# A list scheduler that knows of the SBUF port, of longer scans and of longer matmuls

## The chip, the cores and the metric

The kernel runs on one core of one Trainium2 chip. The metric is the device time of one execution in microseconds; the time before is the median of three runs. The profile is of one more execution on the same kind of chip, taken with the hardware profiler.

## The reference, cut to what matters

Four layers of one trunk over 256 context tokens and 256 latent tokens, model width 1024, all in float32. Each layer has two sub-layers:

```
hg, rw, gates = split(modulate(rms_norm(x), shift, scale) @ w_in)   # 2560 + 1920 + 2048 columns
o_hg = bidirectional HGRN2 (gated linear recurrence, 4 heads of 128)
o_rw = bidirectional RWKV-7 (decay, delta-rule state update, 8 heads of 64, grid-aware token shift)
m = sigmoid(g_hg) * (o_hg @ proj_a) + sigmoid(g_rw) * (o_rw @ proj_b)
x = x + gate * rms_norm(m @ w_out)
x = x + gate * rms_norm((silu(h @ w1_gate) * (h @ w1_up)) @ w2)     # SwiGLU, 2816 wide
```

The shifts, scales and gates come from `silu(c) @ ada_w` (adaLN modulation), for the latent and for the context condition. The recurrences of the context start from zero, and those of the latent tokens from the context's final states. The output is the latent stream after four layers; in the last layer the context goes only as far as its states.

## The kernel before, in words

Activations lie channel-major, 128 channels by 512 tokens (context, then latent) in a tile. A float32 product is made of three fast ones: weights and activations are each split into a rounded part (`wh`, `hh`) and the rest (`wl`, `hl`), and `mm3` adds wh x hh, wh x hl and wl x hh in PSUM. Weights come from DRAM in pieces of 128x512 (`wr`); ScalarE (ACT) makes `wh`, and GpSimd (POOL) or VectorE (DVE) makes `wl = wr - wh`.

In the mixing stage several streams run together: for each of four pairs of RWKV heads a preparation (`rw_pair`), a solver of unit triangular matrices (`rw_solve`: 30 steps on VectorE with tiles `XS` and `S`, then small matmuls) and a state chain over eight chunks (`rw_chain`: c_ps matmuls, `S0P` on GpSimd, updates of `UV` and `S` on VectorE); for each of four HGRN2 heads seven levels of a decay tree (`hg_head`: `hX`, `hY` on VectorE, `SF`, `PF`, `PB`, `SB` on GpSimd); and the gate projections. Then come the merge, the output projection and SwiGLU, big matmuls with simple work around them. The modulation of the next layer (`ada_pair`: sums of 128x512 products on VectorE) is spread over that.

The order of the instructions is not written by hand. `body` records every instruction in a `Plan`: a node with its engine (or "any": VectorE or GpSimd), what it must wait for, and a cost in nanoseconds from `Plan.cost`. `Plan.schedule` then runs a list schedule over five queues (pe, act, vec, pool, dma): at each step the engine that can start first takes, of its ready nodes, the one with the highest rank (the longest chain of costs and lags that hangs on it, plus a bias of its stream); `LOOK` lets an engine wait shortly for a better node. `emit` issues the instructions in the order of their planned starts, and on the chip every engine runs its own list in that order. `PAR` (when each stream is recorded), `BIAS` and `LOOK` are constants that were chosen for this kernel. The costs that matter here, before:

```python
# pe, float32r operands; n columns of output, m of weights
return max(n / 2.4, m / 1.2) + 2.5
# vec
two = name in ("tensor_scalar", "tensor_copy") and not psum
return 67.0 + n * (0.53 if two else 1.042) + 61.0 * ptr
# pool, tensor_scalar with a scalar from memory
return 686.0
```

Nothing in the plan before says that VectorE and GpSimd can hold each other up.

Of the kernel before, what the change touches and what calls it, by code (L numbers as in the profile page):

```python
# [14 lines left out]
PSUM = bass.MemoryType.PSUM  # L15

P = 128
D = 1024
NK = 8
T = 512  # L20
# [51 lines left out]
MAXLOOK = 200  # L72
WINDOW, COLD = 4096 / 1.2, (0.39, 0.87)
# [10 lines left out]
class Node:  # L84
    """One instruction, or several of an engine in a row, with what it waits for."""
# [3 lines left out]
    def __init__(self, engs, calls, preds, costs, load, kind):  # L89
        self.engs, self.calls, self.preds, self.costs, self.load, self.kind = engs, calls, preds, costs, load, kind  # L90


class Plan:
    """Takes down the kernel's instructions, and emits them in the order of a list schedule: each engine runs, of what
    could start, what the longest chain of work hangs on."""
# [10 lines left out]
    def lo(self, i):  # L106
        """The engine of the weights' second parts."""
        return self.any if LO[i] else self.pool

    def tile(self, pool, shape, dt, tag, bufs, name):  # L110
        """A tile; one of a tag takes the place of the one that its tag gave out bufs tiles before."""
        if not tag:
            t = pool.tile(shape, dt, name=name)
            self.tiles[t.tensor.name] = ([], [], ())
            return t
        t = pool.tile(shape, dt, tag=tag, name=name, bufs=bufs)
        held = self.tags.setdefault((id(pool), tag), [])
        held.append(t.tensor.name)
        old = self.tiles.pop(held.pop(0)) if len(held) > bufs else ([], [])
        self.tiles[t.tensor.name] = ([], [], {x for x, _ in old[0] + old[1]})  # L120
        return t

    @staticmethod
    def region(a):
        """Partitions and elements that an access pattern spans."""
        ap, off = a.ap, a.offset
        sp = str(a.space)
        if sp.endswith("PSUM"):
            return 0, 128, 0, 1
        if sp.endswith("SB"):  # L130
            row, n = ap[0]
            p0, off, rest = off // row, off % row, ap[1:]
        else:
            p0, n, rest = 0, 1, ap
        lo = off + sum(min(0, s * (c - 1)) for s, c in rest)
        hi = off + sum(max(0, s * (c - 1)) for s, c in rest) + 1
        return p0, p0 + n, lo, hi

    def together(self):
        """The instructions recorded in this context, all of one engine, stay one after another."""  # L140
        @contextmanager
        def group():
            self.gang = -1
            yield
            self.gang = None
        return group()

    def add(self, engs, name, args, kw):
# [6 lines left out]
        preds = set()  # L155
# [16 lines left out]
        preds.discard(n)  # L172
        b = 4
# [3 lines left out]
        if join:  # L177
            x = self.nodes[n]
            x.calls.append((name, args, kw))
            x.preds |= preds  # L180
            x.costs[0] += costs[0]
        else:
            load = b / DMA_RATE if engs[0] == "dma" else 0.0
            if engs[0] == "pe":
                load = args[1].ap[0][1] / P * (0.37 if out.start_partition() and out.shape[0] <= C else 1.0)
            self.nodes.append(Node(engs, [(name, args, kw)], preds, costs, load, self.kind))
# [8 lines left out]
    @staticmethod  # L195
    def cost(eng, name, out, args, kw):
        """Nanoseconds that an instruction holds its engine."""
        n = 1
# [7 lines left out]
        if eng == "pe":  # L206
            w = args[1].ap
            m = 1
            for x, c in w[1:]:
                m *= c  # L210
            if name == "transpose":
                return max(m / 1.2, 107.0)
            if args[1].dtype == F32R:
                return max(n / 2.4, m / 1.2) + 2.5
            if m == n and m <= 64:
                return (0.9 if out.start_partition() else 1.75) * m
            n = 2 * n / 2.4 * (0.44 if n == 512 and out.ap[0][1] == 32 else 1.0)
            return 2 * (max(n, m / 1.2) + 2.5)
        if eng == "act":
            return (51.0 if psum else 93.0) + n * 0.833 + 93.0 * bool(ptr)  # L220
        if eng == "vec":
            if name == "memset":
                return n * 1.05
            two = name in ("tensor_scalar", "tensor_copy") and not psum
            return 67.0 + n * (0.53 if two else 1.042) + 61.0 * ptr
        if name == "memset":
            return 35.0 + 0.833 * n
        if name == "tensor_scalar":
            if ptr:
                return 686.0  # L230
# [10 lines left out]
    def schedule(self):  # L241
# [26 lines left out]
        tail = 1e9  # L268

# [8 lines left out]
        while len(order) < N:  # L278
# [26 lines left out]
            _, i = heapq.heappop(ready[e])  # L305
            x = nodes[i]
            on[i] = e
            c = x.costs[x.engs.index(e)]
# [43 lines left out]
def body(ctx, tc, xT, cc, ada_w, w_in, rw_lo, rw_g2, proj_a, proj_b, w_out, ffn_w1, ffn_w2,  # L352
# [122 lines left out]
    def load_split(src, k0, nk, c0, ncol, place=None):  # L475
        """Weight rows k0*128.. and columns c0.. as its rounded part and the rest."""
# [24 lines left out]
    def psum2(w, src, hi, lo, rg=slice(0, T), tag="s"):  # L501
        """PSUM tile with w^T src for w of zeros and ones, src going in two parts."""
# [7 lines left out]
    def spots(tile):  # L510
        """Places for the split weights of one output tile in [P, 4, T]."""
# [7 lines left out]
    def proj(src, nk, c0, xh, xl, t0, place=None):  # L519
        """PSUM tile with W[:, c0:c0+128]^T x for tokens t0.., with a place for the weights stream by stream."""  # L520
# [24 lines left out]
    def norms(xs, t0, post=None, pre=None):  # L545
        """x += G * rms_norm(y), and then h = rms_norm(x) * A + B per channel and stream, split in two parts."""
# [79 lines left out]
    def ada_put(pm, b, n, ps):  # L626
        """Sums of n blocks of columns from b on, each stream's in 128 / 2 n rows, put channel-major in md."""
# [12 lines left out]
    def ada_first(l, pm):  # L640
        """The first four blocks of 512 columns of silu(c) @ ada_w[l], each in a quarter of the rows."""
# [14 lines left out]
    def ada_pair(l, pm, b):  # L656
        """Blocks b and b + 1, the products summed over the rows of each partition first."""
# [22 lines left out]
    def ada_finish(pm, i):  # L680
        """Scale, shift and gate of sub-layer i // 3 with the norm weights in."""
# [31 lines left out]
    def sigm(o, src, nb, t):  # L713
        """o = sigmoid(src - nb) by exp and ln; t is all of o."""
# [5 lines left out]
    def shifted(ps, j, lmu, t0, tag):  # L720
        """pf = p + mu (shift(p) - p) of projection tile j."""
# [20 lines left out]
    def layer(l, pm, xs, xd, hh, hl):  # L742
# [32 lines left out]
        def stacked(src, tags):  # L775
            """Per direction src's rounded part and the rest, in the two halves of the rows."""
# [204 lines left out]
        def rw_solve(p):  # L981
            """Inverses of pair p's unit triangular matrices, 32 x 32 blocks first."""
# [44 lines left out]
        def rw_chain(p):  # L1027
            """Pair p's state chain, and the outputs of the chunks that both directions have reached."""
# [73 lines left out]
            # group norm  # L1102
# [24 lines left out]
        def hg_head(e):  # L1127
# [55 lines left out]
            def score(h, xx, yy):  # L1183
                """Products of the tokens of a block of 64 with each other or, for h = 64, with the block beside."""
# [105 lines left out]
        def gate_tiles():  # L1290
            """Sigmoids of the gates, to DRAM."""
# [58 lines left out]
        def branch(br, j):  # L1350
            """Branch br's gated part of tile j, and with the second one the sum."""
# [89 lines left out]
    def ada_to(l, i, n=1000):  # L1441
        """At most n more pieces of the modulation, up to the first i parts of layer l."""
# [72 lines left out]
```

## Time and profile before

| | |
|---|---|
| time, median of 3 runs | 4484.12 us (4477.95 to 4488.85) |
| span of the profiled execution | 4491.0 us, which is its own time as far as the page tells; 6.9 us above the median |
| TensorE (PE) busy | 4151.3 us, 92% |
| VectorE (DVE) busy | 3314.2 us, 74% |
| ScalarE (ACT) busy | 2161.3 us, 48% |
| GpSimd (POOL) busy | 2318.9 us, 52% |
| mean granted TensorE clock | 0.924 |

PE is the row of matmuls and PEld that of weight loads, which overlap them. All instructions have one source line, that of `emit` (L341), so groups are told apart by the tiles that they write and read, as `out<-in`. The span's stages, by the times of the weights' transfers and the norms: mixing of layers 0 to 3 in 75 to 676, 1268 to 1892, 2440 to 3063 and 3612 to 4187 us; merge, output projection and SwiGLU between and after them.

### The profile page before, as it was taken

Reading aid. Unit: us, or ns where it says so; the run is one execution under the profiler, and the core shown is the slowest. Engines: PE = TensorE matmul, PEld = TensorE weight load, DVE = VectorE, ACT = ScalarE, POOL = GpSimd, SP = SyncE. Lnnn points to the kernel's source line nnn. Section 1 sums busy time; section 2 is a strip of 40 time slices with the busy share of each in tenths; the row PEclk is TensorE's granted clock in tenths of the full one; section 3 lists DMA queues with packets and bytes.
Section 4 is the critical chain, followed back from the end, with each engine's and each line's share of the span. In section 5 each row is a group of like instructions: output and inputs, shape, how many; then the busy total and the mean of one; then the engine's idle time right before and its main releaser. Section 6 shows DMA issues by size and latency. Waiting matters only on the chain. (4 is left out here: it accounts for less than half of the span.)

```text
span 4491.0 us, 72501 instructions
## 1 busy us (share of the span) xinstructions
PE 4151.3 (92%) x26290; PEld 3248.2 (72%) x26290; DVE 3314.2 (74%) x5772; ACT 2161.3 (48%) x4458; POOL 2318.9 (52%) x2121
## 2 busy tenths in 40 slices
PE   7999998899999999989999999999899989888998
PEld 5676776677777767778777676677777766667888
DVE  5988878977388898676627988876754487887665
ACT  4554653433255565534434554554433354554564
POOL 2464654465445456454654554554555535455542
PEclk8998899999998998899999998899999988887999
DMA  4211127455421111354433211116444421111555
GB/s 151 59 46 36 51 88 227 140 166 158 134 73 57 49 44 46 125 173 125 139 114 122 63 49 41 46 56 205 122 146 124 137 67 43 41 44 39 159 151 162
DMA packets 661415, 451.08 MB, mean 100 GB/s; under 512 B 28224, under 2 KB 584256, under 8 KB 661056
## 3 DMA queue, kind: packets, MB, share of 16 engines
q1 hardware_dynamic: 661056, 446.44, 33.1%
q8 instruction: 207, 3.39, 0.3%
q14 instruction: 152, 1.25, 0.1%
HBM read 416.98 MB, written 29.36 MB: 99 GB/s over the span
## 5 line engine op out<-in xcount | busy, mean ns | idle before, releaser
L341 POOL TENSOR_TENSOR wl<-wr,wh 128x512 fp32r<-128x512 f32 x726 | 1017.5, 1404 | 1034.3 <-ACT wh L341 705.9
L341 PE MATMUL p_ps<-hh,wh 128*128 128x512 f32 (+1 forms) x2784 | 1073.7, 398 | 30.2 <-ACT wh L341 15.8
L341 PE MATMUL p_ps<-hh,wl 128*128 128x512 f32 (+1 forms) x2784 | 1053.1, 397 | 30.9 <-POOL wl L341 21.4
L341 PE MATMUL p_ps<-hl,wh 128*128 128x512 f32 (+1 forms) x2784 | 1060.0, 394 | 0.0
L341 ACT ACTIVATE wh<-wr 128x512 fp32r<-128x512 f32 x986 | 610.0, 621 | 844.3 <-PE p_ps L341 678.8
L341 PEld LDWEIGHTS p_ps<-hh,wl 128*128 128x128 f32 x2784 | 544.5, 198 | 157.8 <-POOL wl L341 46.9
L341 PEld LDWEIGHTS p_ps<-hh,wh 128*128 128x128 f32 x2784 | 541.9, 197 | 145.2 <-ACT wh L341 26.9
L341 PEld LDWEIGHTS p_ps<-hl,wh 128*128 128x128 f32 x2784 | 543.4, 198 | 97.0 <-issue 9.2
L341 POOL TENSOR_SCALAR fn<-fn 128x512 f32<-128x512 f32 (+1 forms) x152 | 230.9, 1519 | 177.4 <-ACT fn L341 168.8
L341 DVE TENSOR_TENSOR fn<-fn,p_ps 128x512 f32<-128x512 f32 (+1 forms) x208 | 127.1, 614 | 219.9 <-ACT fn L341 129.0
L341 POOL TENSOR_SCALAR S0P<-S,pcs 128x64 f32<-128x64 f32 x192 | 156.7, 829 | 222.0 <-DVE S L341 221.2
L341 DVE TENSOR_TENSOR wl<-wr,wh 128x512 fp32r<-128x512 f32 x260 | 186.9, 723 | 101.1 <-ACT wh L341 59.7
L341 DVE TENSOR_TENSOR XS<-XS,S 64x30 f32<-64x30 f32 (+14 forms) x480 | 214.0, 446 | 10.8
L341 ACT ACTIVATE fn<-fn 128x512 f32<-128x512 f32 (+1 forms) x304 | 174.3, 574 | 89.7 <-POOL fn L341 84.9
L341 DVE TENSOR_TENSOR S<-XS 64x30 f32<-64x30 f32 (+14 forms) x480 | 207.3, 432 | 10.8
L341 PE MATMUL s_ps<-XS,X8b 64*64 64x64 f32 (+2 forms) x1024 | 147.2, 298 | 23.2 <-ACT X8a L341 14.5
L341 POOL TENSOR_TENSOR SF<-SF,PF 128x256 f32<-128x256 f32 x112 | 90.9, 812 | 139.0 <-ACT hY L341 138.2
L341 PEld LDWEIGHTS s_ps<-XS,X8b 64*128 64x128 f32 (+1 forms) x1024 | 118.9, 196 | 55.2 <-ACT X8a L341 24.1
L341 PE MATMUL s_ps<-XS,BK 64*64 64x64 f32 (+2 forms) x1024 | 139.2, 275 | 13.3 <-DVE XS L341 12.6
L341 PEld LDWEIGHTS s_ps<-XS,BK 64*128 64x128 f32 (+1 forms) x1024 | 107.9, 175 | 58.9 <-issue 37.1
L341 DVE SCALAR_TENSOR_TENSOR UV<-c_ps,pcs,S0P 64x64 f32<-64x64 f32 x384 | 108.6, 283 | 56.1 <-PE c_ps L341 45.6
L341 PE MATMUL p_ps<-SC,wh 128*128 128x512 f32 (+1 forms) x440 | 143.4, 363 | 2.4 <-ACT SC L341 2.2
(525 smaller groups left out, 9554.7 us busy)
## 6 DMA issues: line engine op xcount, KB each, us to landing
wr<-ffn_w SPq DMA_DIRECT2D x512, 256.0 KB, 3.0
wr<-w_in SPq DMA_DIRECT2D x408, 256.0 KB, 2.9
hq<-ada_w SPq DMA_DIRECT2D x242, 256.0 KB, 2.9
PB<-ada_w SPq DMA_DIRECT2D x110, 256.0 KB, 3.0
wr<-w_out SPq DMA_DIRECT2D x64, 256.0 KB, 3.0
gts<-fn SPq DMA_DIRECT2D x48, 256.0 KB, 3.0
wr<-proj_a SPq DMA_DIRECT2D x32, 256.0 KB, 4.5
wr<-proj_b SPq DMA_DIRECT2D x32, 256.0 KB, 3.8
```

The costliest lines, as they stand in the source:

```text
L341: getattr(self.eng[self.on[i]], name)(*args, **kw)
```

## The change

No instruction is changed. The scheduler's model of time gets new parts. `on_port` marks nodes that use the port to SBUF that VectorE and GpSimd share: on GpSimd tensor_tensor and tensor_copy, on VectorE operations with all operands in SBUF that have two inputs or are a tensor_scalar, copy or transpose. In the schedule such a node begins no sooner than the port is free; where that would be over `PORT` (100 ns) away, the engine looks at up to 12 ready nodes for one that needs no port and ends within `OVER` (200 ns) of the port's release, and takes it first. A VectorE node whose output starts in another group of 32 partitions than the last one's costs 88 ns more. A float32r matmul of 512 columns goes from 215.8 to 228.9 ns, a scan of 512 columns from 600 to 1132, a 1024-column transpose from 1134 to 1193, a GpSimd tensor_scalar with a scalar from memory from 686 to 440. Docstrings and comments are blanked; the lines of the diff that only do that are left out here.

```diff
+PORT, OVER = 100.0, 200.0
...
+    def __init__(self, engs, calls, preds, costs, load, kind, port, quad):
         self.engs, self.calls, self.preds, self.costs, self.load, self.kind = engs, calls, preds, costs, load, kind
+        self.port, self.quad = port, quad
...
+            self.nodes.append(Node(engs, [(name, args, kw)], preds, costs, load, self.kind,
+                                   [self.on_port(e, name, out, args, kw) for e in engs], r[0] // 32 if engs[0] == "vec"
+                                   else None))
...
+    def on_port(eng, name, out, args, kw):
+
+        if eng not in ("vec", "pool"):
+            return False
+        ins = [x for x in (kw.get(k) for k in ("in_", "in0", "in1", "data0", "data1", "data")) if hasattr(x, "space")]
+        ins = ins or [x for x in args[1:] if hasattr(x, "space")]
+        if eng == "pool":
+            return name in ("tensor_tensor", "tensor_copy")
+        if not all(str(x.space).endswith("SB") for x in [out] + ins):
+            return False
+        return len(ins) > 1 or name in ("tensor_scalar", "tensor_copy", "transpose")
...
-                return max(n / 2.4, m / 1.2) + 2.5
+                return max(n / 2.35 + 11.0, m / 1.2 + 2.5)
...
+            if name in ("transpose", "tensor_tensor_scan"):
+                return 67.0 + n * (1.1 if name == "transpose" else 2.08)
...
-                return 686.0
+                return 440.0
...
-            _, i = heapq.heappop(ready[e])
+            r0, i = heapq.heappop(ready[e])
             x = nodes[i]
+            n = x.engs.index(e)
+            if x.port[n] and port > t + PORT:
+                held = [(r0, i)]
+                while ready[e] and len(held) < 12:
+                    r0, i = heapq.heappop(ready[e])
+                    held.append((r0, i))
+                    y = nodes[i]
+                    if on[i] or y.port[y.engs.index(e)] or t + y.costs[y.engs.index(e)] > port + OVER:
+                        continue
+                    break
+                else:
+                    r0, i = held[0]
+                for h in held:
+                    if h[1] != i:
+                        heapq.heappush(ready[e], h)
+                x = nodes[i]
+                n = x.engs.index(e)
             on[i] = e
-            c = x.costs[x.engs.index(e)]
+            c = x.costs[n]
+            if x.quad is not None and e == "vec":
+                if x.quad != quad:
+                    t += 88.0
+                quad = x.quad
+            if x.port[n]:
+                t = max(t, port)
+                port = t + c
```

## Rows read from the trace of the kernel before

**Rows 1.** The page: busy us, share of the span, instructions.

```profile
PE 4151.3 (92%) x26290; PEld 3248.2 (72%) x26290; DVE 3314.2 (74%) x5772; ACT 2161.3 (48%) x4458; POOL 2318.9 (52%) x2121
```

**Rows 2.** Windows, one per stage: stretch, length, busy us by engine, clock, DMA.

```profile
core 0: us, PE busy (x) PEld busy (x) DVE busy (x) ACT busy (x) POOL busy (x), PEclk, DMA share, GB/s
75.00:676.00 601.00, 566.98 (x4262) 423.96 (x4261) 511.30 (x972) 333.68 (x719) 334.86 (x343) 0.92 0.19 56
676.00:1268.00 592.00, 532.35 (x2447) 417.14 (x2446) 433.54 (x575) 216.69 (x391) 305.81 (x217) 0.97 0.54 161
1268.00:1892.00 624.00, 593.03 (x4366) 443.40 (x4365) 515.87 (x1001) 343.56 (x742) 331.71 (x341) 0.91 0.19 58
1892.00:2440.00 548.00, 517.32 (x2393) 417.78 (x2392) 325.36 (x440) 213.24 (x386) 298.69 (x219) 0.97 0.47 142
2440.00:3063.00 623.00, 591.92 (x4365) 442.21 (x4364) 515.86 (x1000) 343.54 (x742) 331.84 (x342) 0.91 0.19 59
3063.00:3612.00 549.00, 512.54 (x2386) 411.42 (x2385) 324.65 (x436) 212.69 (x383) 300.13 (x221) 0.98 0.47 142
3612.00:4187.00 575.00, 518.86 (x3697) 403.01 (x3696) 474.15 (x936) 304.05 (x697) 305.72 (x340) 0.82 0.17 50
4187.00:4491.00 304.00, 273.10 (x2188) 262.88 (x2187) 183.79 (x316) 168.57 (x350) 106.10 (x90) 0.95 0.56 164
```

**Rows 3.** Waits of TensorE: who waited for whom, us in total, times, longest.

```profile
PE s_ps L341 <- ACT fn L341: 35.6, 23, 5.4
...
PE c_ps L341 <- DVE S L341: 24.1, 30, 2.3
PE p_ps L341 <- POOL wl L341: 23.6, 39, 1.9
PE s_ps L341 <- DVE XS L341: 21.2, 9, 4.8
...
PE g_ps L341 <- DVE hY L341: 14.9, 13, 3.6
```

**Rows 4.** Timeline of VectorE from 1500 us: start, duration, operation.

```profile
1501.85 0.41 DVE L341 TENSOR_TENSOR hY<-hY,kf 128x256 f32<-128x256 f32 x1
...
1503.12 1.34 DVE L341 TENSOR_TENSOR hY<-hY,kb 128x256 f32<-128x256 f32 x1
```

**Rows 5.** Timeline of GpSimd in the same stretch.

```profile
1502.89 1.29 POOL L341 TENSOR_TENSOR BK<-X8a,BK 128x512 fp32r<-128x512 f32 x1 [1.14 <-ACT BK L341]
```

**Rows 6.** Groups by form, VectorE: count, busy us, mean ns, idle before.

```profile
L341 DVE SCALAR_TENSOR_TENSOR y<-hq,cvec,y 128x512 f32<-128x512 f32 x110 | 116.0, 1055 | 2.3 <-DMA hq<-ada_w 2.1
...
L341 DVE TENSOR_TENSOR hX<-hX,hq 128x512 f32<-128x512 f32 x128 | 111.0, 868 | 4.4 <-ACT hX L341 3.9
L341 DVE SCALAR_TENSOR_TENSOR UV<-c_ps,pcs,S0P 64x64 f32<-64x64 f32 x384 | 108.6, 283 | 56.1 <-PE c_ps L341 45.6 <-ACT fn L341 2.0 <-ACT wh L341 0.9
L341 DVE TENSOR_TENSOR fn<-fn,p_ps 128x512 f32<-128x512 f32 x156 | 105.5, 680 | 203.1 <-ACT fn L341 113.1 <-PE p_ps L341 88.9
...
L341 DVE TENSOR_TENSOR_SCAN X4c<-rmk,X8a 128x512 f32<-128x512 bf16 x32 | 44.2, 1381 | 5.8 <-ACT X8a L341 5.8
```

**Rows 7.** Windows, a stretch of SwiGLU in layer 0.

```profile
898.00:1010.00 112.00, 104.13 (x455) 80.31 (x454) 87.14 (x103) 42.70 (x73) 68.20 (x45) 1.00 0.56 165
```

**Rows 8.** Timeline around the chain in layer 3, VectorE.

```profile
3916.01 1.17 DVE L341 SCALAR_TENSOR_TENSOR UV<-c_ps,pcs,S0P 64x64 f32<-64x64 f32 x4
...
3917.20 0.48 DVE L341 SCALAR_TENSOR_TENSOR S<-c_ps,pcs,S0P 128x64 f32<-128x64 f32 x2
```

**Rows 9.** Groups by form, GpSimd.

```profile
L341 POOL TENSOR_SCALAR S0P<-S,pcs 128x64 f32<-128x64 f32 x192 | 156.7, 829 | 222.0 <-DVE S L341 221.2
```

**Rows 10.** The tile S0P: durations min/median/max in ns, first and last start.

```profile
L341 POOL TENSOR_SCALAR S0P<-S,pcs x192: 433/632/2887, 232.3 to 4187.1; 128x64 f32<-128x64 f32 x192
```

More of the change, by code (lines that the diff above doesn't have):

```diff
@@ L87 @@
     head = tail = 0.0
-    def __init__(self, engs, calls, preds, costs, load, kind):
+    def __init__(self, engs, calls, preds, costs, load, kind, port, quad):
         self.engs, self.calls, self.preds, self.costs, self.load, self.kind = engs, calls, preds, costs, load, kind
+        self.port, self.quad = port, quad
 class Plan:
@@ L172, in add @@
         preds.discard(n)
+        r = (out.start_partition(),) if hasattr(out, "start_partition") else (0,)
         b = 4
@@ L185, in add @@
                 load = args[1].ap[0][1] / P * (0.37 if out.start_partition() and out.shape[0] <= C else 1.0)
-            self.nodes.append(Node(engs, [(name, args, kw)], preds, costs, load, self.kind))
+            self.nodes.append(Node(engs, [(name, args, kw)], preds, costs, load, self.kind,
+                                   [self.on_port(e, name, out, args, kw) for e in engs], r[0] // 32 if engs[0] == "vec"
+                                   else None))
         if engs[0] == "pe":
@@ L193, in add @@
             x.tail = m / 1.2 if m == b // (4 * out.ap[0][1]) and m <= C else 1e9
+    @staticmethod
+    def on_port(eng, name, out, args, kw):
[8 more added lines that the diff above has]
+        return len(ins) > 1 or name in ("tensor_scalar", "tensor_copy", "transpose")
     @staticmethod
@@ L268, in schedule @@
         tail = 1e9
+        port, quad = 0.0, 0
         def release(i):
```

## The prediction

> **What bounds the kernel now.** I read the page first: on one core, TensorE is busy 92% of a span of 4491.0 us, VectorE 74%, GpSimd 52% [rows 1]. That average mixes stages, so the next view is the busy time by stage [rows 2]. Each layer has a token-mixing stage, then a stage of merge, output projection and SwiGLU. The reader is to see two different limits. In the four mixing stages (601, 624, 623 and 575 us) TensorE is idle for 34, 31, 31 and 56 us, VectorE is busy for 82 to 85%, and the granted clock is 0.92, 0.91, 0.91 and 0.82. In the other stages of layers 0 to 2 the clock is 0.97 or 0.98 and VectorE has slack (73%, then 59%). TensorE is thus the bound everywhere, but in the mixing stages it is short of work now and then, and slow: at full clock the same stages lack 0.08 x 601 + 0.09 x 624 + 0.09 x 623 + 0.18 x 575 = 264 us.
>
> The third view is what TensorE waits for [rows 3]. All its idle time is 4491.0 - 4151.3 = 340 us. Some groups sit at norms, where nothing else is ready (the squares that ACT makes, 35.6 us). Others are in the mixing stages and wait for VectorE or GpSimd: the chain's state S 24.1 us, the weights' second part from GpSimd 23.6 us, the solver's XS 21.2 us, HGRN2's hY 14.9 us. Together 83.8 us. These four are what an order of instructions can reach.
>
> **The change part by part.** No instruction is added, removed or altered in size; all that moves is the order on each engine and, for operations recorded on "any", which of VectorE and GpSimd runs them. Every engine runs in order, so what a better order saves is seen only where the engine that sets the end waits. The four parts of the new model are each set against a row.
>
> (1) The port. A VectorE product of two SBUF operands, hY 128x256, takes 0.41 us at 1501.85; the same one at 1503.12 takes 1.34 us [rows 4]. In between GpSimd began a subtraction at 1502.89 that holds until 1504.18 [rows 5]; 1503.12 + 1.34 = 1504.46, so VectorE's product ran after it, not beside it. The group views say the same in the mean: hX <- hX,hq, both operands in SBUF, 868 ns; fn <- fn,p_ps, of the same shape with one operand in PSUM, 680 ns [rows 6]. That is 188 ns for each of 128. The planner before lets both engines run at once and costs each at 67 + 512 x 1.042 = 600 ns; the new one lets one wait for the other, and where VectorE would wait over 100 ns it looks for one of the next ready instructions that needs no port. So the port is real here, and the new plan places VectorE's results later, where they are.
>
> (2) Longer scans and matmuls. The scan was planned at 600 ns and is now 67 + 512 x 2.08 = 1132; the trace has 1381 in the mean [rows 6], port waits included. The 512-column matmul was 512 / 2.4 + 2.5 = 215.8 ns and is now 512 / 2.35 + 11 = 228.9. In a stretch at full clock 455 matmuls keep TensorE busy 104.13 us [rows 7], 228.9 ns each. The new figure is the measured one; the plan's TensorE gets 6% slower.
>
> (3) The 88 ns where a VectorE output starts in another group of 32 partitions than the one before. Four UV updates that alternate between the halves take 1.17 us, 0.29 each; two S updates of as many columns, both from partition 0, take 0.48 us, of which the second needs some 0.20 after the first [rows 8]. Planned before: 67 + 64 x 1.042 + 61 = 195 ns; 195 + 88 = 283. This agrees too.
>
> (4) GpSimd's scaling S0P, 686 ns in the plan, is now 440. The trace has a mean of 829 [rows 9], and 433 at least, 632 in the median, 2887 at most [rows 10]: 440 is what it takes undisturbed. On average the plan is here further off than before, by 686 - 440 = 246 ns.
>
> What a truer plan is worth no row shows directly, so I bound it. **Waits:** of the 83.8 us of [rows 3], nothing to all of it can go. I take half, 42 us: no row splits such a wait into the part that a truer order avoids and the part that is dependence, and a value in the middle is at most 42 us off either way. **Clock:** a TensorE with fewer pauses may be granted more of its 2.4 GHz rather than 1.2. Between layer 1's mixing stage (31 us idle, 5.0%, clock 0.91) and layer 3's (56 us, 9.8%, 0.82), 4.8 points of idle time go with 9 points of clock, about 1.9 us of clock for one of idle [rows 2]; but layer 0's stage has more idle time than layer 1's and no lower clock. So between 0 and 1.9 x 42 = 80 us, and I take a quarter of a microsecond for one, 10 us, nearer the end that the second pair shows. **Shuffling:** all else in the order changes with it, at start times and biases (PAR, BIAS, LOOK) that stay. The nearest row: layers 0 and 1 have the same start times and other orders, and their mixing stages take 601 and 624 us, 23 us apart. Layers 1 and 2 are of one order in the trace (the same counts, 624 and 623), so they go together: sqrt(46^2 + 23^2 + 23^2) = 56 us either way. I take 0 and keep 56 on both sides for the range. **The other stages** I cost at nothing: matmuls follow one another there, and VectorE's 1055 ns for the modulation's 128x512 sums [rows 6] lies beside them. Were that cover gone, 110 of them at about 300 ns over an undisturbed one would be 33 us in each such group.
>
> Sum: 42 + 10 + 0 = 52 us, 4491 - 52 = 4439 for the span. The profiled span is 6.9 us above the median of the runs shown (4484.12), so the time is about 4432 us, 1.2% less. A measurement of this kernel can tell about 0.2%, 9 us, from no change.
>
> **The rivals.** *Hidden anyway (no change).* TensorE is the bound at 92%, and its waits for VectorE are a fiftieth of the span; the collisions are on an engine with slack. Then only the place of the waits changes: 4484, within 4475 to 4493. Against it: the mixing stages, where VectorE is busy five sixths of the time and TensorE does wait for it.
>
> *The shuffle loses (slower).* The place is the four mixing stages, the price the 23 us that separate two orders at the same start times [rows 2]. If each of the four becomes longer by that, 92 us stand against the gain of 52: 4432 + 92 = 4524. It decides from 61 us on, that is when three of four go the wrong way. For it: constants such as 46.8 or 185.1 belong to one order, and to dodge a collision that is planned to 100 ns, real times must keep to the plan that closely, while S0P alone spreads from 433 to 2887 ns [rows 10]. Against it: the new costs agree with the rows, and an order made on false costs is not better for being the older.
>
> *S0P too cheap (the gain is eaten).* The new model keeps GpSimd's scalings off the port and shortens S0P. If S0P were last to arrive at the update that reads it, 192 x 246 ns = 47 us of lateness would come in: 4432 + 47 = 4479, about no change; without any gain, 4531. Against it: VectorE's UV update, which reads S0P, is idle before it 56.1 us in all, of which 45.6 end with TensorE's c_ps; S0P is not among the releasers that the row names [rows 6]. The Trainium skill (SBUF — State Buffer, section Who interferes with whom) says that a VectorE instruction with two SBUF inputs contends with any GpSimd instruction that reads SBUF, which takes in the scalings that this change leaves off the port. S0P's spread of durations agrees with that rule; by it, this rival has a cause in the hardware, with the price worked out above.
>
> **How the numbers follow.** The forecast (fewer waits, faster by over 0.2%) 0.64; hidden 0.11; S0P 0.03; the shuffle loses 0.22. So faster 0.64, within 0.2% 0.14, slower 0.22. The forecast's own range is 4379 (all 84 us of waits and 21 of clock: 4484 - 105) to 4475. The range for the time takes in no change and the lighter half of the slower case, and on the fast side some of a lucky shuffle: 4370 to 4515; below it and above it about 2 in 10 together.
>
> **What would show it.** Port: the mean of hX <- hX,hq falls from 868 ns towards 680, and VectorE's busy time with it. Waits: the four groups of TensorE's waits fall from 83.8 to some 42 us. Stages: the mixing stages of layers 1 and 2 from 624 to about 612 us, layer 3's from 575 to about 560, with a clock above 0.91 and 0.82; the others as they were within 10 us. S0P: TensorE's or VectorE's waits name S0P if its cost was the mistake. The prediction is wrong if VectorE gets less busy and TensorE's idle time stays (hidden), or if waits of a new kind, for ACT or for GpSimd's weights, take the place of those on VectorE, or if the clock of the mixing stages falls (the shuffle).

## The result, and the profile after

The changed kernel is slower: 4671.9 us in the median of four runs (4655.23 to 4680.99) against 4486.5 us for the kernel before on the same chip, a ratio of 1.039 [1.034, 1.043]. The forecast was 4432 us, the range 4370 to 4515. The profiled execution has a span of 4672.4 us, 181 us more than before's 4491.0 [rows 2].

The page of the changed kernel, its span, its busy times (us, share of the span, instructions) and its clock in 40 slices, answering to [rows 1]:

```profile
span 4672.4 us, 72587 instructions
...
PE 4241.3 (91%) x26290; PEld 3341.9 (72%) x26290; DVE 3258.5 (70%) x5650; ACT 2166.0 (46%) x4458; POOL 2447.0 (52%) x2243
...
PEclk8968797999999787799999978887999996776899
```

TensorE runs the same 26290 matmuls and is busy 90 us longer (4241.3 - 4151.3) and idle 91 us longer (431 - 340). VectorE is less busy (3258.5 for 3314.2), and 122 of its instructions went over to GpSimd. So it is not VectorE's load that grew.

To compare stage by stage I cut both spans at the norms, which both kernels have: mixing and merge, then SwiGLU, for each layer. Windows of the kernel before, with columns as in [rows 2]:

```profile
57.00:837.00 780.00, 715.39 (x4932) 537.66 (x4932) 669.70 (x1194) 401.41 (x849) 415.59 (x400) 0.92 0.28 86
837.00:1263.00 426.00, 396.65 (x1870) 315.57 (x1870) 282.81 (x374) 156.90 (x280) 225.19 (x162) 0.99 0.49 144
1263.00:2019.00 756.00, 713.20 (x4908) 540.12 (x4908) 610.26 (x1129) 399.98 (x847) 408.81 (x397) 0.92 0.26 80
2019.00:2435.00 416.00, 396.90 (x1846) 320.81 (x1846) 230.96 (x311) 156.76 (x279) 221.59 (x163) 0.97 0.44 129
2435.00:3190.00 755.00, 711.15 (x4908) 537.47 (x4908) 609.31 (x1127) 399.78 (x846) 409.26 (x397) 0.92 0.26 80
3190.00:3608.00 418.00, 394.66 (x1846) 317.49 (x1846) 232.21 (x312) 157.32 (x279) 222.71 (x165) 0.98 0.44 129
3608.00:4283.00 675.00, 601.35 (x4308) 476.99 (x4308) 540.39 (x1056) 358.76 (x820) 347.22 (x375) 0.84 0.23 67
4283.00:4491.00 208.00, 193.89 (x1588) 192.19 (x1588) 121.55 (x205) 116.36 (x232) 64.60 (x55) 0.96 0.54 158
```

The same windows of the changed kernel:

```profile
57.00:897.00 840.00, 752.55 (x4932) 569.41 (x4932) 641.15 (x1158) 404.11 (x848) 446.28 (x426) 0.85 0.26 78
897.00:1309.00 412.00, 393.55 (x1870) 317.29 (x1870) 288.27 (x378) 157.40 (x281) 237.79 (x164) 0.99 0.51 153
1309.00:2116.00 807.00, 747.93 (x4908) 569.14 (x4908) 597.97 (x1104) 401.43 (x847) 428.32 (x422) 0.85 0.24 74
2116.00:2522.00 406.00, 390.95 (x1846) 317.40 (x1846) 238.02 (x312) 157.08 (x278) 229.38 (x168) 0.98 0.45 136
2522.00:3328.00 806.00, 735.05 (x4908) 561.20 (x4908) 595.12 (x1089) 400.91 (x847) 435.21 (x426) 0.86 0.24 74
3328.00:3741.00 413.00, 392.13 (x1846) 317.46 (x1846) 238.76 (x317) 158.66 (x280) 231.22 (x171) 0.98 0.45 133
3741.00:4457.00 716.00, 606.38 (x4308) 488.08 (x4308) 529.63 (x1028) 360.59 (x820) 362.06 (x397) 0.79 0.22 65
4457.00:4672.00 215.00, 195.18 (x1588) 191.83 (x1588) 112.22 (x199) 111.78 (x231) 72.76 (x60) 0.97 0.51 149
```

The matmul counts agree window by window, so the stages hold the same TensorE work. The four mixing stages lose 60 + 51 + 51 + 41 = 203 us; the SwiGLU stages give 14, 10 and 5 back and the last one loses 7, so 22 us come back and 181 remain. In the mixing stages TensorE is busy 101 us longer for the same matmuls (2842 for 2741), with the clock down from 0.92 to about 0.85 in layers 0 to 2 and from 0.84 to 0.79 in layer 3, and idle 102 us longer (327 for 225). Half of the loss is idle time and half is a slower TensorE.

Who TensorE waits for, after (us in total, times, longest), answering to [rows 3]:

```profile
PE c_ps L386 <- DVE S L386: 56.7, 42, 3.0
PE s_ps L386 <- ACT fn L386: 42.7, 23, 7.9
PE p_ps L386 <- POOL wl L386: 40.0, 43, 4.1
...
PE s_ps L386 <- DVE XS L386: 15.1, 12, 6.0
...
PE g_ps L386 <- DVE hY L386: 8.9, 9, 5.1
```

The four groups that were to fall from 83.8 to 42 us rose to 56.7 + 40.0 + 15.1 + 8.9 = 120.7 us. The solver's XS and HGRN2's hY fell, by 12.1 us together. The state chain's S more than doubled and the weights' second part from GpSimd grew by 16.4. The prediction put all four in the mixing stages, but of that last group's 23.6 us before only 6.3 fall there. Within the mixing windows alone the four go from 66.6 to 110.4 us.

### The profile page after: what moved, and what is told of

Read it like the earlier page. It is cut to its first block, busy times and chain, and to the rows that moved or that the text cites. A ratio compares the mean times of both kernels' runs of the same rounds, so it can differ in the third digit from the quotient of the medians.

```text
span 4672.4 us, 72587 instructions
## 1 busy us (share of the span) xinstructions
PE 4241.3 (91%) x26290; PEld 3341.9 (72%) x26290; DVE 3258.5 (70%) x5650; ACT 2166.0 (46%) x4458; POOL 2447.0 (52%) x2243
## 5 line engine op out<-in xcount | busy, mean ns | idle before, releaser
L386 POOL TENSOR_TENSOR wl<-wr,wh 128x512 fp32r<-128x512 f32 (+1 forms) x833 | 1146.7, 1381 | 1168.6 <-ACT wh L386 737.8
L386 POOL TENSOR_SCALAR S0P<-S,pcs 128x64 f32<-128x64 f32 x192 | 145.8, 772 | 190.5 <-DVE S L386 189.9
L386 DVE TENSOR_TENSOR XS<-XS,S 64x30 f32<-64x30 f32 (+14 forms) x480 | 227.8, 475 | 10.6
L386 DVE TENSOR_TENSOR S<-XS 64x30 f32<-64x30 f32 (+14 forms) x480 | 220.9, 460 | 10.5
L386 DVE TENSOR_TENSOR wl<-wr,wh 128x512 fp32r<-128x512 f32 (+1 forms) x153 | 111.8, 731 | 116.1 <-ACT wh L386 105.0
L386 POOL COPY SC<-XS 64x256 f32<-64x256 f32 x128 | 69.3, 542 | 222.8 <-DVE SC L386 220.2
L386 DVE SCALAR_TENSOR_TENSOR UV<-c_ps,pcs,S0P 64x64 f32<-64x64 f32 x384 | 108.6, 283 | 100.6 <-PE c_ps L386 75.2
L386 PE MATMUL s_ps<-XS,BK 64*64 64x64 f32 (+2 forms) x1024 | 152.8, 298 | 8.5 <-DVE XS L386 5.1
L386 PEld LDWEIGHTS s_ps<-XS,BK 64*128 64x128 f32 (+1 forms) x1024 | 121.8, 195 | 51.6 <-issue 30.3
L386 DVE TENSOR_TENSOR SC<-s_ps,scm 128x512 f32<-128x512 f32 (+1 forms) x128 | 83.9, 655 | 101.2 <-PE s_ps L386 67.9
```

The source lines that it names most:

```text
L386: getattr(self.eng[self.on[i]], name)(*args, **kw)
```

## Where it happens: the solver and the chain behind it

`rw_solve` has 60 VectorE steps for each pair of heads (two instructions for each of its 30 rounds), each needing the one before, on tiles in SBUF, so in the new plan these steps wait for the port. A timeline of VectorE in the kernel before, layer 1 (start, duration, operation):

```profile
1351.67 0.31 DVE L341 TENSOR_TENSOR S<-XS 64x150 f32<-64x150 f32 x1
1352.02 0.69 DVE L341 TENSOR_TENSOR SC<-s_ps,scm 128x512 f32<-128x512 f32 x1
1352.74 0.32 DVE L341 TENSOR_TENSOR XS<-XS,S 64x150 f32<-64x150 f32 x1
```

The same two steps in the changed kernel:

```profile
1405.50 0.31 DVE L386 TENSOR_TENSOR S<-XS 64x150 f32<-64x150 f32 x1
1408.19 0.69 DVE L386 TENSOR_TENSOR wl<-wr,wh 128x512 fp32r<-128x512 f32 x1 [2.38 <-ACT wh L386]
1408.90 0.69 DVE L386 TENSOR_TENSOR SC<-s_ps,scm 128x512 f32<-128x512 f32 x1
1409.62 0.31 DVE L386 TENSOR_TENSOR XS<-XS,S 64x150 f32<-64x150 f32 x1
```

Between step and step there were 1.07 us before and are 4.12 now. The next step could run at 1405.81, but VectorE runs its list in order, and a `wl` stands ahead of it in the list that has to wait 2.38 us for ACT. Over the whole solver of this pair, and over the chain that begins after it, the windows show the same (columns as in [rows 2]). Before:

```profile
1340.00:1387.00 47.00, 44.87 (x198) 31.60 (x197) 41.45 (x87) 23.61 (x49) 21.18 (x20) 1.00 0.23 67
1437.00:1494.00 57.00, 56.28 (x496) 40.54 (x495) 50.03 (x125) 25.47 (x69) 35.60 (x45) 0.97 0.13 38
```

After:

```profile
1392.00:1490.00 98.00, 93.75 (x466) 70.89 (x466) 87.54 (x143) 56.85 (x110) 59.99 (x50) 0.97 0.26 77
1508.00:1571.00 63.00, 57.57 (x450) 43.73 (x449) 47.05 (x131) 23.00 (x64) 29.51 (x39) 0.64 0.04 11
```

The first line of each is the solver: 87 VectorE instructions in 47 us became 143 in 98. The 60 steps are the same, so the 27 other instructions there became 83. This pair is the extreme one. Over the four pairs of layer 1 the other instructions between first and last step went from 356 to 394, and the time from 297 to 398 us: the steps themselves take 101 and 113 us of it, the other instructions 177 and 223, and VectorE is idle for 19 and 63. So the waits of what stands between the steps count for as much as its work. TensorE is not idle during the first solver (93.75 of 98 us): it runs on with projections. These are then missing later. The second line is the first state chain, and the clock there is 0.64 for 0.97. The windows of the projections (p_ps) alone say why the chain stands bare; columns are us, PE busy (count), clock, DMA share, GB/s, first for the stretch ahead of the first chain, then for that chain, then for the last ones of the layer. Before:

```profile
1349.00:1437.00 88.00, 56.05 (x205) 0.88 0.22 64
1437.00:1494.00 57.00, 27.95 (x90) 0.97 0.13 38
1719.00:1877.00 158.00, 75.92 (x241) 0.92 0.20 62
```

After:

```profile
1395.00:1508.00 113.00, 84.28 (x329) 0.94 0.27 79
1508.00:1571.00 63.00, 8.42 (x24) 0.64 0.04 11
1807.00:1989.00 182.00, 60.05 (x215) 0.75 0.19 60
```

Ahead of the first chain there were 205 projection matmuls and are 329; beside it 90 and 24; beside the last ones 241 in 158 us and 215 in 182. The chain's own matmuls are small and each hangs on an update of VectorE. With few big matmuls in between, TensorE waits (c_ps on S), and its granted clock there is 0.64 for 0.97 and 0.75 for 0.92.

## The experiments

The theory at first was that the port's part of the plan is at fault; the rivals were that the longer matmul cost is, that the search for a node to put first (the dodge) is, and that any other order would lose as much. All ratios are to the kernel before on the same chip, with 95% intervals.

**The port taken out of the changed kernel, and the port alone.** The first edit keeps all new costs:

```diff
             if x.port[n]:
-                t = max(t, port)
-                port = t + c
+                pass
```

> The changed kernel, but the scheduler lets VectorE and GpSimd run side by side again (no wait for the port and so no dodging); the longer matmuls and scans, the 88 ns and the cheaper S0P stay. Port theory (the planned wait for the port makes VectorE's results look late, the plan then puts the big projections in front of the state chains, and the chains run bare at a lower clock): the time is back near the kernel before, 4450 to 4540 us, and the first chain of layer 1 again has some 90 projection matmuls beside it at a clock over 0.9. Cost theory (the 6% longer matmuls lengthen the ranks against the fixed biases): the time stays at 4630 to 4700 us. Shuffle theory (any other order at the old constants loses): anything between 4500 and 4700, with no tie to the chains.

The second keeps the port and puts the costs of before back (this edit is called *old costs* from here on):

```diff
-                return max(n / 2.35 + 11.0, m / 1.2 + 2.5)
+                return max(n / 2.4, m / 1.2) + 2.5
...
-            if name in ("transpose", "tensor_tensor_scan"):
+            if False:
...
-                return 440.0
+                return 686.0
...
-                    t += 88.0
+                    t += 0.0
```

> The port part alone: the old costs of matmul, scan, transpose, S0P and no 88 ns, but the planned wait for the port and the dodging stay. Port theory: 4630 to 4720 us, with the first chain of layer 1 bare (some 24 projection matmuls, clock near 0.65). Cost theory: 4450 to 4540 us. Shuffle theory: between 4500 and 4700.

Without the port 4562.3 us, 1.013 [1.010, 1.016]; the port alone 4617.0 us, 1.025 [1.022, 1.029]. Each of the two halves loses by itself, the port the more. Both times lie outside what the port theory expected, in the range left to the shuffle. Its sign in the first chain of layer 1 did come: between the chain's first and last `S0P` there are 21 projection matmuls at a clock of 0.62 with the port alone, and 55 at 0.91 without it (72 at 0.96 before, 24 at 0.70 in the changed kernel).

**No dodge, and the matmul cost alone.** The first is the changed kernel, the second is the kernel before:

```diff
-PORT, OVER = 100.0, 200.0
+PORT, OVER = 1e12, 200.0
```

> The changed kernel without the dodging: a node waits for the port in the plan, but no other node is taken in its place. Port theory: the planned wait is enough, 4640 to 4720 us. Dodge theory (taking lower ranked nodes first delays what the chain hangs on): back to 4450 to 4540 us.

```diff
-                return max(n / 2.4, m / 1.2) + 2.5
+                return max(n / 2.35 + 11.0, m / 1.2 + 2.5)
```

> The kernel before with one number changed, the planned cost of a 512-column matmul from 215.8 to 228.9 ns. Port theory: 4450 to 4530 us, and what it differs from the kernel before is the size of a shuffle without the port. Cost theory: 4600 us or more.

Without the dodge 4652.0 us, 1.032 [1.029, 1.035]: the dodge is not the cause. The matmul cost alone, which is the measured 228.9 ns, gives 4617.3 us, 1.025 [1.022, 1.029], where the cost theory had put it. That a right cost loses as much as the port alone called for a measure of how much any change of order moves the time.

**A cost changed by next to nothing**, in the kernel before, VectorE's and then the matmul's:

```diff
-            return 67.0 + n * (0.53 if two else 1.042) + 61.0 * ptr
+            return 68.0 + n * (0.53 if two else 1.042) + 61.0 * ptr
```

> The kernel before with a change of cost that means nothing: VectorE's fixed part 67 becomes 68 ns. No port, no longer matmul. Tuned-order theory (the order before is one good one among many that almost equal costs give, and any other loses 1 to 2.5%, as the matmul cost alone did): 4530 to 4620 us. Port and cost theory (only costs that differ by several per cent move the time): 4470 to 4515 us.

```diff
-                return max(n / 2.4, m / 1.2) + 2.5
+                return max(n / 2.4, m / 1.2) + 2.6
```

> The kernel before with the planned 512-column matmul at 215.9 in place of 215.8 ns. Tuned-order theory: 4530 to 4620 us. Port and cost theory: 4470 to 4515 us.

One nanosecond on VectorE: 4525.3 us, 1.005 [1.003, 1.007]. A tenth of one on the matmul: 4489.9 us, 0.998 [0.996, 1.000]. The first lies between the two ranges expected, the second in the lower one. So half a per cent can come from a change that says nothing about the chip.

**Which engine's planned waits.** In the changed kernel only GpSimd waits and dodges; the other kernel has "vec" in the place of "pool":

```diff
-            if x.port[n] and port > t + PORT:
+            if e == "pool" and x.port[n] and port > t + PORT:
...
-                t = max(t, port)
-                port = t + c
+                if e == "pool":
+                    t = max(t, port)
+                port = max(port, t + c)
```

> The changed kernel, but in the plan only GpSimd waits for the port (and only GpSimd dodges); VectorE's planned times are free of it. Port theory, in the form that VectorE's late results make the plan put big projections before the chains: as without the port, 4530 to 4590 us, and the last chain of layer 1 ends some 620 us after the stage's first norm. If GpSimd's waits did it (weights' second parts and S0P planned late): 4620 to 4700 us, chains ending at 660 to 680 us.

> The changed kernel, but in the plan only VectorE waits for the port (and only VectorE dodges). Port theory in VectorE's form: 4620 to 4700 us, with the last chain of layer 1 ending 650 to 690 us after the first norm and a clock under 0.88 in that stage. If GpSimd's waits did it: 4530 to 4590 us.

GpSimd alone 4542.5 us, 1.011 [1.007, 1.015], with a clock of 0.925; VectorE alone 4619.5 us, 1.026 [1.022, 1.030], with 0.897, the first within the port theory's range and the second at its lower end. The loss of clock goes with VectorE's waits.

**The plan's own model of a slow TensorE**, which both kernels have: could it be what the longer costs upset?

```diff
-                if cold:
+                if False:
```

> The changed kernel with one line of the old model taken out: the plan's TensorE never drops to its lower clock (no doubled costs). If the plan's own clock is what turns port waits into a worse order (planned waits make the planned TensorE cold, its work looks twice as long, and the order is fitted to that): 4500 to 4600 us and a granted clock of over 0.90. If the port waits themselves place the big projections ahead of the chains: 4630 to 4700 us and a clock near 0.88.

4752.7 us, 1.059 [1.055, 1.062], above either expectation: that model is not the cause, and without it the order is worse.

**The small costs alone**, that is the changed kernel without the port and with the old matmul cost:

```diff
-                return max(n / 2.35 + 11.0, m / 1.2 + 2.5)
+                return max(n / 2.4, m / 1.2) + 2.5
...
-                t = max(t, port)
-                port = t + c
+                pass
```

> The changed kernel without the port and with the old matmul cost: scans, transposes, the 88 ns and S0P alone. With the matmul cost at 1.025 and all costs without the port at 1.013, two answers are open. If these small costs repair part of what the matmul cost spoils: 4420 to 4480 us. If each is one more draw of an order: 4490 to 4560 us.

4540.0 us, 1.010 [1.007, 1.013], in the range of one more draw of an order.

**The port for nodes outside the streams of the mixing stage alone, and inside alone**, both with old costs; kind "A" is the modulation:

```diff
-                                   [self.on_port(e, name, out, args, kw) for e in engs], r[0] // 32 if engs[0] == "vec"
+                                   [(self.kind is None or self.kind[0] == "A") and self.on_port(e, name, out, args, kw) for e in engs], r[0] // 32 if engs[0] == "vec"
```

> The old costs, and the port known to the plan only for what is recorded outside the streams of the mixing stages (merge, output projection, SwiGLU, norms, modulation). In the runs so far the stages after the mixing were shorter wherever VectorE waited for the port in the plan (layers 0 to 2: 409, 409 and 408 us with the port alone, against 426, 416 and 418 before), and the mixing stages were longer. If the two effects go apart by stage: the three SwiGLU stages near 410 us, the mixing stages within 10 us of the kernel before, and 4440 to 4480 us in all, faster than both kernels. If the gain belongs to the mixing order that comes before: 4490 us or more.

The other kernel has `self.kind is not None and self.kind[0] != "A" and` in that place.

> The complement: the old costs, and the port known to the plan only inside the streams of the mixing stages. If the loss lies there: 4610 to 4680 us, the mixing stages of layers 1 and 2 at 790 to 810 us between the norms against 756 before, the SwiGLU stages as before. If the loss needs the whole: 4480 to 4560 us.

Outside: 4461.9 us, 0.993 [0.991, 0.995], faster than both kernels. Inside: 4670.3 us, 1.039 [1.037, 1.042], the whole loss of the change without any of its other costs. One mixing and one SwiGLU window of each, layer 1; the port outside:

```profile
1236.00:1993.00 757.00, 706.61 (x4908) 537.92 (x4908) 605.34 (x1112) 400.26 (x847) 414.95 (x406) 0.92 0.26 78
1993.00:2399.00 406.00, 390.35 (x1846) 316.84 (x1846) 232.93 (x315) 157.02 (x278) 232.63 (x169) 0.98 0.45 136
```

The port inside:

```profile
1328.00:2146.00 818.00, 740.77 (x4908) 568.25 (x4908) 599.53 (x1104) 401.41 (x847) 433.25 (x421) 0.85 0.25 74
2146.00:2562.00 416.00, 397.41 (x1846) 321.01 (x1846) 230.49 (x312) 157.16 (x279) 222.61 (x163) 0.97 0.44 129
```

The outside part keeps the 10 us that SwiGLU gains (406 for 416) and leaves mixing at 757 for 756; the inside part has the long mixing stage (818) and SwiGLU as before (416). The two halves of the change are apart here. The 0.7% gained outside is no larger than what a change of order can move by itself, but the SwiGLU stages of all three layers are shorter (411, 406 and 408 us for 426, 416 and 418).

**Which stream inside: the solver** (kind "Z"). The changed kernel with all its new costs, where only the solver neither waits for the port nor holds it:

```diff
-                                   [self.on_port(e, name, out, args, kw) for e in engs], r[0] // 32 if engs[0] == "vec"
+                                   [(self.kind is None or self.kind[0] != "Z") and self.on_port(e, name, out, args, kw) for e in engs], r[0] // 32 if engs[0] == "vec"
```

> The changed kernel, but the solver's instructions (rw_solve, 60 dependent VectorE steps for each pair) neither wait for the port nor hold it in the plan. Solver theory (a planned wait before each step makes the plan put other work between the steps, the solver of pair 0 in layer 1 takes 98 us for 47 and its chain starts 25 us later): the solver of pair 0 is back under 60 us, the chains start as before, and the time is 4500 to 4570 us, that of all costs without the port (ratio 1.013) less some 30 us that the port gains in the SwiGLU stages. Spread theory (the port waits of all streams do it together): 4600 to 4680 us.

4456.8 us, 0.992 [0.989, 0.995]: this one exemption takes away the whole loss, and more than was expected (4500 to 4570). The solver of pair 0 in layer 1, expected under 60 us, takes 81. Its windows of layer 1 and 2:

```profile
1254.00:2013.00 759.00, 718.54 (x4908) 543.38 (x4908) 604.56 (x1111) 401.59 (x846) 418.34 (x414) 0.90 0.26 79
2013.00:2421.00 408.00, 391.95 (x1846) 317.99 (x1846) 238.68 (x315) 157.88 (x278) 230.32 (x168) 0.98 0.45 134
2421.00:3156.00 735.00, 693.34 (x4908) 523.54 (x4908) 596.02 (x1100) 402.22 (x847) 429.49 (x420) 0.95 0.26 81
3156.00:3563.00 407.00, 390.26 (x1846) 316.84 (x1846) 237.76 (x311) 157.88 (x279) 232.41 (x171) 0.98 0.45 135
```

and its wait of the chain for S:

```profile
PE c_ps L386 <- DVE S L386: 12.6, 19, 2.1
```

Mixing is at 759 and 735 us for 807 and 806, the clock at 0.90 and 0.95 for 0.85 and 0.86, and the wait for S at 12.6 us for 56.7 (24.1 before). GpSimd runs 2225 instructions here, 104 of the 122 that it took over in the changed kernel, so that move of work is not the cause. The edit takes two things out of the plan, the solver's waits and its hold of the port against GpSimd. The hold is not the cause: where GpSimd alone waits, the solver still holds the port, and the ratio is 1.011, no more than without the port (1.013).

**The same exemption under other costs, and the solver alone.** First the exemption with old costs, then with the old matmul cost only:

```diff
+                                   [(self.kind is None or self.kind[0] != "Z") and self.on_port(e, name, out, args, kw) for e in engs], r[0] // 32 if engs[0] == "vec"
```

> The old costs, the port known to the plan everywhere but in the solver. Solver theory: 4440 to 4500 us, near the kernel that knows of the port outside the mixing alone (ratio 0.993). Spread theory: 4560 to 4640 us, near the port alone (ratio 1.025).

```diff
+                                   [(self.kind is None or self.kind[0] != "Z") and self.on_port(e, name, out, args, kw) for e in engs], r[0] // 32 if engs[0] == "vec"
...
-                return max(n / 2.35 + 11.0, m / 1.2 + 2.5)
+                return max(n / 2.4, m / 1.2) + 2.5
```

> The changed kernel with the solver free of the port, and the matmul cost back at 215.8 ns. If the longer matmul costs something of its own (alone it was 1.025, and it made the last SwiGLU stage 215 to 220 us long for 208): 4420 to 4450 us, the last stage at 206 to 209 us. If it costs nothing beside the port: 4450 to 4480 us, as with the longer matmul (4456.8).

And with old costs, of VectorE only the solver on the port, beside all of GpSimd:

```diff
+                                   [(e == "pool" or self.kind is not None and self.kind[0] == "Z") and self.on_port(e, name, out, args, kw) for e in engs], r[0] // 32 if engs[0] == "vec"
```

> The old costs, and of VectorE's instructions the solver's alone know of the port; GpSimd's all do. Solver theory: 4600 to 4700 us, mixing stages near 800 us, the solver of pair 0 in layer 1 at 80 us or more. Spread theory: 4490 to 4560 us.

The exemption gives 4484.4 us, 0.997 [0.995, 0.999], with old costs, against 1.025 with the solver on the port, and 4520.6 us, 1.003 [1.001, 1.006], with the old matmul cost. That last one was to show whether the matmul cost is a second cause: without it the kernel is not faster but 1.2% slower than with it, above either range expected. The solver alone gives 4576.4 us, 1.018 [1.015, 1.020], between what the two theories expected: it does not make the whole loss without the other streams' waits.

All 16 kernels and the change fall into three groups:

| plan | ratios |
|---|---|
| the solver waits for the port on VectorE | 1.018, 1.025, 1.026, 1.032, 1.039, 1.039, 1.059 |
| VectorE waits for the port, but not in the solver | 0.992, 0.993, 0.997, 1.003 |
| no wait for the port on VectorE | 0.998, 1.005, 1.010, 1.011, 1.013, 1.025 |

A ratio between 1.00 and 1.025 alone says little, since plans without any wait on VectorE give that too. The weight is on the two pairs that differ in the exemption alone: 1.039 and 0.992 with the new costs, 1.025 and 0.997 with the old ones. The first pair is far outside that spread; the 1.025 of the second, taken alone, is not.

Two things in the traces go with it. One is the time from the first to the last step of a solver, added over the four pairs of layer 1 and over all 16 solvers of the four layers. The other is the number of projection matmuls (p_ps) that run between the first and the last `S0P` of a chain, added over all 16 chains:

| kernel | solvers of layer 1, us | all solvers, us | projections beside the chains | ratio |
|---|---|---|---|---|
| port outside the streams | 259 | 1043 | 1205 | 0.993 |
| before | 297 | 1150 | 1322 | 1 |
| solver exempt, new costs | 302 | 1278 | 1250 | 0.992 |
| solver exempt, old costs | 282 | 1159 | 1097 | 0.997 |
| matmul cost alone | 266 | 1072 | 1237 | 1.025 |
| solver alone | 364 | 1491 | 1002 | 1.018 |
| the port alone | 397 | 1511 | 787 | 1.025 |
| the change | 398 | 1504 | 656 | 1.039 |
| port inside the streams | 415 | 1597 | 871 | 1.039 |

Over all kernels, all solvers take 1491 to 1708 us in the seven plans where the solver waits and 1043 to 1283 in the other eleven; the projections are 600 to 1089 and 1097 to 1383. The matmul cost alone has short solvers and many projections and still loses 2.5%, so a plan can lose by another way too.

**What is shown and what is not.** Shown: the loss comes with the planned port waits in the solver, under new costs and under old ones, and goes when the solver is exempt; it lies in the mixing stages, where the solvers become longer and fewer projections stand beside the chains. Argued, from the scheduler's code, is how a planned wait does that:

```python
            if x.port[n]:
                t = max(t, port)
                port = t + c
...
            end = t + c
            free[e] = end
```

A node that waits holds its engine in the plan until its own end, so nothing but the dodge is put into the wait, and without the dodge the loss stays (1.032). What the wait does is to end each step later in the plan. Before the next step, which the plan has ready 127 ns after that end, another node that is ready can be taken, and what hangs on the solver falls behind work that does not. In the real order such nodes stand ahead of the next step even when they are late themselves.

Open: why the matmul cost alone loses 2.5%, when with the solver exempt it loses nothing; and what the other streams' waits add to the solver's (1.039 for 1.018). Not tried: start times, biases and look-ahead (`PAR`, `BIAS`, `LOOK`) chosen anew for the changed plan. They were chosen for the plan before, so no run tells whether a plan that knows of the port would lose with constants of its own. A single solver's length is not the measure either: that of pair 0 in layer 1 takes 81 us with the solver exempt, near the 85 of the solver alone, and only the sum tells the two apart.

## Why the prediction was wrong

**The step that failed** is the term "I take half, 42 us" of the waits, with the 10 us of clock that hung on it. It rested on the thought that a plan with truer costs makes a better order. The four waits rose by 36.9 us, and the mixing stages, which were to go from 624 to about 612 us and from 575 to about 560, went the other way, by 41 to 60 us each (cut at the norms). The sign was lost there. The runs showed what stands in its place: the planned waits pull the steps of the solvers apart (297 us for those of layer 1 became 398), the projections run ahead of the chains in place of beside them, and with the solver exempt from the port the same costs give 0.992. On an engine that runs its list in order, what is ordered between dependent steps delays all that hang on them, and the prediction did not ask for a chain of such steps among the operations that `on_port` marks, though the solver's XS stood among the four waits of [rows 3].

**The shuffle term**, 0 with 56 us either way, was too small. One nanosecond in a cost moved the time by 0.5%, and a cost that is the measured one by 2.5%, 116 us. The 23 us between two orders at the same start times [rows 2] came from stages of one and the same plan, and are no measure of what a new plan can do. Nor are they a difference of order: layer 1's window holds 104 matmuls more than layer 0's (4366 and 4262), TensorE is busy 26 us longer in it and idle 3 us less, so the 23 us are more work in the window.

**The rival "the shuffle loses"** had the sign and the signal (the clock of the mixing stages falls) and gave 4524 us; the time is 148 us above that. It named the constants and the drift from planned times as causes; the runs name another, the solver's planned waits, which it does not have.

**Right, but of little worth:** the port is real and the new costs are nearer the trace, yet the collisions hardly fell. Groups by form in the changed kernel, VectorE, answering to [rows 6]:

```profile
L386 DVE SCALAR_TENSOR_TENSOR UV<-c_ps,pcs,S0P 64x64 f32<-64x64 f32 x384 | 108.6, 283 | 100.6 <-PE c_ps L386 75.2 <-ACT wh L386 4.3 <-ACT he L386 3.4
...
L386 DVE TENSOR_TENSOR hX<-hX,hq 128x512 f32<-128x512 f32 x128 | 105.9, 827 | 3.2 <-ACT hX L386 1.7
```

The mean of hX went from 868 to 827 ns, not towards 680, in a plan in which no two nodes marked for the port overlap. The trace says where the rest comes from: of the 42 products that took over 760 ns, 39 overlap a GpSimd tensor_tensor or copy, which `on_port` marks. So most of it is real times that drift from the plan, and not the operations that are not marked. One reading of the prediction was loose: the product at 1503.12 us ended 0.28 us after GpSimd's subtraction, less than the 0.41 us that it takes undisturbed, so by these times it was held up for most of the subtraction but did not start after it.

**S0P** was rightly put last among the rivals. The UV update's idle time grew from 56.1 to 100.6 us, but S0P is not among the releasers that the row names. The tile's durations after (min/median/max in ns):

```profile
L386 POOL TENSOR_SCALAR S0P<-S,pcs x192: 434/564/3050, 256.2 to 4348.6; 128x64 f32<-128x64 f32 x192
```

Their spread, 434 to 3050 ns, again agrees with the rule of the Trainium skill (SBUF — State Buffer, section Who interferes with whom) that was weighed in the prediction: all 66 scalings of 800 ns or more overlap a VectorE instruction with two SBUF inputs, against 43 of the 90 under 500 ns.

**The other stages, costed at nothing,** gained 29 us in layers 0 to 2. The port outside the streams brings as much by itself (406 us for 416 in layer 1). The last stage lost 7.

**The clock** was priced too low, at a quarter of a microsecond for one of idle time: in the mixing stages 101 us of busy time came with 102 us of idle time, about one for one.

## What to carry to other kernels

A truer cost model need not make a better list schedule. Here planned waits pulled the steps of a dependent chain apart, other work was ordered between them and ahead of what hangs on them, and engines that run their lists in order then had to follow. Before a resource is added to a planner, look for such chains among the nodes that it will delay, and try the plan with them exempt (here 0.992 for 1.039). And change a cost by a nanosecond first: a planner whose time moves by 0.5% then gives no verdict on one such change from one order.

## What the runs showed of the hardware

The clock fell beside a busy TensorE. In the first state chain of layer 1 it is busy 57.57 of 63 us and has a granted clock of 0.64, a mean over its 2.4 and 1.2 GHz; before, the same chain had 56.28 of 57 us at 0.97. The prediction had tied the clock to idle time. Over the mixing stages the two did rise together, 101 us of busy time for the same matmuls and 102 us of idle time. But idle time alone does not set the clock: with the solver exempt, TensorE is idle for 40 us in layer 1's mixing stage and 42 in layer 2's, at 0.90 and 0.95.
